# Last projection of a one-core hybrid block: residual sums and one set of weight differences from GpSimd to VectorE

## The chip, the core and the metric

One core of one Trainium2 chip runs the whole program. The metric is the device time of an execution in microseconds; the kernel before stands at the median of three runs. The engines are called by their names and, in the profile, by short ones: TensorE (PE, its weight loads PEld), VectorE (DVE), ScalarE (ACT), GpSimd (POOL) and SyncE (SP), which issues the DMAs.

## What is computed

One layer of a backbone block over 2048 tokens of width 1024 and 256 context tokens: modulation, norms, an input projection, a Fourier group beside a Mamba-2 scan, an output projection, then a SwiGLU feed-forward. Only its last line matters here, the projection back to width 1024 with a norm, a gate and a residual:

```python
def swiglu(h, w_gate, w_up, w_down):
    return (jax.nn.silu(h @ w_gate) * (h @ w_up)) @ w_down

hx2 = modulate(rms_norm(x, g_pre_ffn[l]), sf_x, cf_x)
x = x + gf_x * rms_norm(swiglu(hx2, w_gate[l], w_up[l], w_down[l]), g_post_ffn[l])
```

All of it is float32; `w_down` is 2816 x 1024.

## The kernel before, in words

**The last projection.** The tokens are worked in two pairs of blocks of 512 tokens (`PAIRS`). For each pair the product with `w_down` is a 2x2 block product done in seven multiplications instead of eight: two token blocks, two halves of the 2816, two halves of the 1024 columns. The seven are named 1 to 7, and `ORDER` gives their sequence: 1, 2, 6, 7, 4, 5, 3 for the first pair and 1, 6, 7, 4, 5, 3, 2 for the second. Below, one of these fourteen is called a position. A position has eleven steps (`f`), and a step has four token tiles of 128 with three matmuls each: operands are split into a high and a low part of a rounded type, and high x high, low x high and high x low are summed. That is 12 matmuls of 128x512 in a step and 132 in a position. The last two steps are run tile by tile.

**What a step needs.** `down_parts` makes a step's two operands up to four steps ahead (`fetch(4)`). The weight block is either a quarter of `w_down` as loaded, or a sum of quarters; it is rounded by ScalarE into `wd` and the remainder is taken by VectorE into the second half of `wd`. The hidden block comes by DMA as `hraw` (512 KB for two steps, four buffers) and is split in the same way into `hd`. So each step costs VectorE two subtractions of 128x512 and ScalarE two casts. Position 6 first changes block 11 in place to block 12 minus block 11 (`sub(G, ...)`, line 904, on GpSimd), then VectorE subtracts the outcome from block 22. Position 7 and position 4 have one difference on GpSimd in each step. In the second pair block 11 lies in the buffers `actC` (first eight steps) and `actB` (last three).

**Finishing a block of tokens.** When a block's sums are complete, `finish` (lines 1787 to 1803) norms them beside the next position: a mean square for four token tiles at once, the inverse root on GpSimd, then for each of eight half tiles of 128x512 VectorE multiplies by the inverse root and the gate (`scalar_tensor_tensor`) and GpSimd adds the saved residual `x2`. `down` draws two pieces from this generator in each step (`steps(run, 2)`, line 1871), so that it is through after six of eleven steps; then one DMA of 2048 KB stores the block. `x2` was loaded by `rows_load` in four DMAs into a buffer of `actC`. Three blocks go this way: the second block of the first pair beside the first pair's last position (here **F1**), its first block beside the second pair's first position (**F2**), and the second pair's second block beside its sixth position (**F3**). The last block ends the program in `finish_last`.

**The order.** For the last projection the order on each engine isn't the written one. The framework's scheduler arranges the instructions of each engine, and the DMAs on SyncE, by its own estimate; each engine then works through its list in that order, and an instruction that waits holds what stands behind it.

Of the kernel before, what the change touches and what calls it, by code (L numbers as in the profile page):

```python
# [17 lines left out]
ALU = mybir.AluOpType  # L18
# [143 lines left out]
def fourier_ssd_block(ctx, tc, a):  # L162
    nc = tc.nc
    pace = Pace()
    V, S, G, T = (Paced(e, n, pace) for e, n in
                  ((nc.vector, "DVE"), (nc.scalar, "ACT"), (nc.gpsimd, "POOL"), (nc.tensor, "PE")))
# [57 lines left out]
    def rsqrt_steps(ssq, n, scale, out):  # L224

        ms = sm.tile([P, n], F32, tag="rq_ms", name="rq_ms", bufs=4)
        V.tensor_scalar(ms, ssq, scale, EPS, ALU.mult, ALU.add)
        yield
        y = sm.tile([P, n], F32, tag="rq_y", name="rq_y", bufs=7)
        G.tensor_tensor(y, ms, mhalf[:, 0:n], op=ALU.pow)  # L230
        out.append(y)
        yield
# [7 lines left out]
    def steps(gen, n=99):  # L240
        for _ in range(n):
            if next(gen, 0) == 0:
                return
# [611 lines left out]
    def qslot(shape, dt=F32):  # L855
        return ff.p3.tile(list(shape), dt, tag="q", name="slot")
# [15 lines left out]
    def hidden_loads(ahead):  # L872

        while hpos[0] < min(hpos[1] + ahead + 1, 14 * ((NJ + 1) // 2)):
            pi, f2 = divmod(hpos[0], (NJ + 1) // 2)
            p, i = divmod(pi, 7)
            n = min(2, NJ - 2 * f2)
            raw = wp.tile([P, 2, 512], F32, tag="raw", name="hraw", bufs=4)
            dma(raw[:, 0:n], hgate_d[p][f2][:, 0:n, PIECE[ORDER[p][i]]])
            hraw[pi, f2] = raw  # L880
            hpos[0] += 1

    def down_parts(p, i, f):

        hpos[1] = (7 * p + i) * ((NJ + 1) // 2) + f // 2
        hidden_loads(3 if f % 2 == 0 else 2)

        def block(b):
            return wblock[p, (b, f // 4)][:, f % 4]

        def temp():
            return ta[0].tile([P, 512], F32, tag="ws", name="wt", bufs=4)

        def sub(engine, out, x, y):
            engine.tensor_tensor(out, x, y, op=ALU.subtract)
            return out

        i_ = ORDER[p][i]
        if i_ in (1, 5):
            src = block(11)  # L900
        elif i_ in (2, 3):
            src = block({2: 21, 3: 22}[i_])
        elif i_ == 6:
            sub(G, block(11), block(12), block(11))
            src = sub(V, temp(), block(22), block(11))
        elif i_ == 7:
            src = sub(G, temp(), block(22), block(12))
        else:
            src = sub(G, temp(), block(11), block(22))
            V.tensor_tensor(src, src, block(21), op=ALU.add)  # L910
        w = wp.tile([P, 2, 512], F32R, tag=("hi", "lo")[pos[1] % 2], name="wd")
        S.copy(w[:, 0], src)
        sub(V, w[:, 1], src, w[:, 0].bitcast(F32))
        raw = hraw[7 * p + i, f // 2][:, f % 2]
        tag, bufs = (("xt", 2), ("sg", 3))[pos[1] // 2 % 2]
        h = ta[0].tile([P, 2, 512], F32R, tag=tag, name="hd", bufs=bufs)
        S.copy(h[:, 0], raw)
        sub(V, h[:, 1], raw, h[:, 0].bitcast(F32))
        return w, h
# [6 lines left out]
    def next_w():  # L926
        fetch(4)
        pos[0] += 1
        return ready.pop(pos[0] - 1)
# [414 lines left out]
    with tc.manual_schedule(engines=ordered):  # L1344
# [232 lines left out]
        ff = SimpleNamespace()  # L1577
# [164 lines left out]
        run = gate_up(0, xs0, beside, last0)  # L1742
# [34 lines left out]
    half = [slice(0, 512), slice(512, D)]  # L1777
# [5 lines left out]
    def rows_load(p, r):  # L1783
        ff.x2 = act("C", F32, (P, 4, D))
        b = PAIRS[p][r]
        for t in range(4):
            dma(ff.x2[:, t], x2_d[4 * b + t])

    def finish(p, r, o, sq):

        ss = ta[0].tile([P, 4], F32, tag="fss", name="fss", bufs=2)
        V.tensor_tensor(ss, sq[:, :, 0], sq[:, :, 1], op=ALU.add)
        rs = []
        for _ in rsqrt_steps(ss, 4, 1.0 / D, rs):
            yield
        for t in range(4):
            for n in range(2):
                oh = o[:, t, half[n]]
                V.scalar_tensor_tensor(oh, oh, rs[0][:, t : t + 1], gffn[n], ALU.mult, ALU.mult)
                G.tensor_tensor(oh, oh, ff.x2[:, t, half[n]], op=ALU.add)  # L1800
                yield
        b = PAIRS[p][r]
        dma(out_d[4 * b * P : 4 * (b + 1) * P, :].rearrange("(t p) d -> p t d", p=P), o)
# [29 lines left out]
    def schedule(p):  # L1833

        at = {}
        if p == 0:
            at = {(0, 2): (0, 12, 0), (0, 5): (0, 12, 1), (0, 8): (0, 22, 0), (1, 1): (0, 22, 1), (1, 4): (0, 12, 2), (1, 7): (0, 22, 2),
                  (4, 2): (1, 11, 0), (4, 6): (1, 11, 1), (5, 2): (1, 12, 0), (5, 6): (1, 12, 1), (5, 9): (1, 11, 2),
                  (6, 0): (1, 12, 2), (6, 3): (1, 22, 0), (6, 7): (1, 22, 1)}
            rows = {(5, 4): 1, (6, 10): 0}  # L1840
        else:
            at = {(0, 3): (1, 22, 2), (1, 0): (1, 21, 2), (1, 3): (1, 21, 0), (1, 6): (1, 21, 1)}
            rows = {(4, 4): 1, (6, 2): 0}
        return at, rows

    def down(p, prev):
        at, rows = schedule(p)
        order = ORDER[p]
        run = prev
        for pos_, i in enumerate(order):  # L1850
            begin, keep = i in (1, 6, 7, 5), i in (2, 4, 3)
            if begin:
                banks = [pb.tile([P, 512], F32, tag="b", name="b") for _ in range(4)]
                if i == 1:
                    first = banks
            acc = first if i == 2 else banks
            end = p == 1 and pos_ == 6
            tail = 4 if end else 2
            f = 0
            while f < NJ:  # L1860
                m = tail if f == NJ - tail else 1
                ws = [next_w() for _ in range(m)]
                for t in range(4):
                    for df, (w, h) in enumerate(ws):
                        for n, (hi_, wi) in enumerate(((0, 0), (1, 0), (0, 1))):
                            T.matmul(acc[t], h[:, hi_, t * P : (t + 1) * P], w[:, wi], start=begin and f == 0 and n == 0,
                                     stop=f + df == NJ - 1 and n == 2, skip_group_check=keep)
                for ff_ in range(f, f + m):
                    if (pos_, ff_) in at:
                        down_load(*at[pos_, ff_])  # L1870
                    steps(run, 2)
                    if (pos_, ff_) in rows:
                        rows_load(p, rows[pos_, ff_])
                f += m
            steps(run)
            run = idle
            if i == 1:
                ff.o1 = qslot((P, 4, D))
                sq1, sq2 = (ta[0].tile([P, 4, 2], F32, tag="fsq", name="fsq", bufs=3) for _ in range(2))
            if i == 7:  # L1880
                ff.o2 = qslot((P, 4, D))
            if end:
                return finish_last(p, ff.o1, sq1, acc)
            for t in range(4):
                u1, u2 = ff.o1[:, t, half[1]], ff.o2[:, t, half[1]] if hasattr(ff, "o2") else None
                ps = acc[t]
                if i == 1:
                    S.copy(u1, ps)
                elif i == 6:
                    V.tensor_tensor(u1, u1, ps, op=ALU.add)  # L1890
                elif i == 7:
                    V.tensor_tensor(u2, u1, ps, op=ALU.add)
                elif i == 4:
                    c = ff.o2[:, t, half[0]]
                    V.tensor_tensor(c, u1, ps, op=ALU.add)
                    squares(c, sq2, t, 0)
                elif i == 5:
                    V.tensor_tensor(u2, u2, ps, op=ALU.add)
                    squares(u2, sq2, t, 1)
                elif i == 3:  # L1900
                    V.tensor_tensor(u1, u1, ps, op=ALU.add)
                    squares(u1, sq1, t, 1)
                    if p == 1:
                        V.tensor_tensor(u1, u1, gffn[1], op=ALU.mult)
                else:
                    c = ff.o1[:, t, half[0]]
                    S.copy(c, ps)
                    squares(c, sq1, t, 0)
            if i == 5:
                run = finish(p, 1, ff.o2, sq2)  # L1910
        return finish(p, 0, ff.o1, sq1)
# [27 lines left out]
```

## Time and profile before

| | |
|---|---|
| median of three runs | 2409.01 us (2407.45 to 2411.35) |
| the profiled execution | 2409.39 us, its span 2407.6 us |
| TensorE busy | 2281.4 us (95%) |
| VectorE busy | 1669.3 us (69%) |
| ScalarE busy | 1113.6 us (46%) |
| GpSimd busy | 1049.4 us (44%) |
| last projection | from 1952.44 us of the span to its end |

In the profile's views `out<-in` names the tiles that an instruction writes and reads, `x` is a count, and a bracket tells how long the engine stood idle just before and who ended that. `slot` is the tile of finished sums, `actC` holds in turn weight blocks and the residual `x2`, `b` is a PSUM bank. A row of windows gives for each engine its busy time and in brackets its instructions, then the granted TensorE clock, the DMA engines' busy share and GB/s.

### The profile page before, as it was taken

To read this page: it belongs to the slowest core of one execution; us is meant where nothing else is said; L and a number is where in the kernel's file an instruction comes from. 1 tells how busy PE (TensorE), PEld (TensorE's weight loads), DVE (VectorE), ACT (ScalarE), POOL (GpSimd) and SP (SyncE) were. 2 spreads that over 40 slices of the span, in tenths; PEclk is the share of its full clock that TensorE was granted. 3 is DMA by queue.
4 is the path that set the end of the run, shared out by engine and by line. 5 is a ranking of instruction groups with operands and counts; after the bars stand their busy time and mean duration, and the time that the engine had idled before them with its cause. 6 is when DMAs were issued, how large, how long until landed. Compare 5 with 4: busy or idle time off the path is not lost. (4 is left out here: it accounts for less than half of the span.)

```text
span 2407.6 us, 30176 instructions
## 1 busy us (share of the span) xinstructions
PE 2281.4 (95%) x10861; PEld 1865.9 (77%) x10861; DVE 1669.3 (69%) x2255; ACT 1113.6 (46%) x2017; POOL 1049.4 (44%) x667
## 2 busy tenths in 40 slices
PE   7999798999989999988999999899999999998998
PEld 3887667777778888876788888788888878876786
DVE  3559878588976888887555555855555665778666
ACT  4535453355428677765623333333323335444354
POOL 2121536635552444443454555355554541425512
PEclk9999998999999999998999999999999999999999
DMA  9355435445466888842333333433333373547333
GB/s 310 129 158 156 131 120 186 147 152 177 152 214 226 263 257 252 256 168 90 121 97 110 106 105 105 149 113 97 109 97 102 105 268 117 186 140 262 95 123 118
DMA packets 272580, 377.20 MB, mean 157 GB/s; under 512 B 17111, under 2 KB 190115, under 8 KB 269358
## 3 DMA queue, kind: packets, MB, share of 16 engines
q1 hardware_dynamic: 243062, 344.49, 44.7%
q10 hardware_dynamic: 29368, 30.78, 3.7%
q8 instruction: 86, 1.41, 0.3%
q14 instruction: 64, 0.52, 0.1%
HBM read 280.49 MB, written 94.72 MB: 156 GB/s over the span
## 5 line engine op out<-in xcount | busy, mean ns | idle before, releaser
L140 PE MATMUL b<-wd,hd 128*128 128x512 f32 x1848 | 429.5, 394 | 15.9 <-DVE hd L140 10.8
L140 PEld LDWEIGHTS b<-wd,hd 128*128 128x128 f32 x1848 | 350.1, 190 | 95.1 <-DVE hd L140 13.5
L140 PE MATMUL mm<-slot,wa 128*128 128x512 f32 x1584 | 378.6, 392 | 10.5 <-ACT sg L140 6.6
L140 PEld LDWEIGHTS mm<-slot,wa 128*128 128x128 f32 x1584 | 297.6, 189 | 75.7 <-ACT sg L140 7.4
L140 DVE SCALAR_TENSOR_TENSOR acc<-u,convw,acc 128x992 f32<-128x992 f32 (+5 forms) x228 | 310.5, 1366 | 23.5 <-ACT acc L140 19.1
L140 POOL TENSOR_TENSOR ws<-raw 128x512 f32<-128x512 f32 x88 | 127.4, 1448 | 310.3 <-DMA raw<-in_w_up_dram 131.4
L140 PE MATMUL mm<-actC,wa 128*128 128x512 f32 x984 | 241.5, 394 | 7.4 <-DVE u L140 7.2
L140 PE MATMUL mm<-actB,wa 128*128 128x512 f32 x1020 | 239.4, 390 | 0.0
L140 PE MATMUL mm<-actA,hi 128*128 128x512 f32 x704 | 227.7, 404 | 3.8 <-DVE actA L140 2.7
L140 ACT CAST wa<-ws 128x512 fp32r<-128x512 f32 x176 | 109.2, 621 | 252.9 <-PE mm L140 215.2
L140 PEld LDWEIGHTS mm<-actC,wa 128*128 128x128 f32 x984 | 186.6, 190 | 47.6 <-issue 8.7
L140 PEld LDWEIGHTS mm<-actB,wa 128*128 128x128 f32 x1020 | 191.2, 188 | 39.6
L140 DVE TENSOR_TENSOR wa<-ws,wa 128x512 fp32r<-128x512 f32 x176 | 156.9, 893 | 59.3 <-ACT wa L140 56.3
L140 POOL TENSOR_TENSOR rq_y<-rq_ms,mhalf 128x1 f32<-128x1 f32 (+2 forms) x60 | 43.1, 723 | 288.6 <-DVE rq_ms L140 274.5
L140 DVE TENSOR_TENSOR u<-u,mm 128x512 f32<-128x512 f32 x126 | 86.4, 686 | 116.4 <-PE mm L140 116.4
L140 DVE TENSOR_TENSOR wa<-raw,wa 128x512 fp32r<-128x512 f32 x132 | 118.4, 898 | 65.2 <-ACT wa L140 64.7
L140 ACT CAST wa<-raw 128x512 fp32r<-128x512 f32 x132 | 82.3, 624 | 163.1 <-PE mm L140 147.7
L140 PEld LDWEIGHTS mm<-actA,hi 128*128 128x128 f32 x704 | 130.1, 191 | 33.4 <-issue 3.7
L140 POOL TENSOR_TENSOR adacc<-adacc,adaw 128x1024 f32<-128x1024 f32 x28 | 74.1, 2648 | 181.8 <-ACT adaw L140 169.8
L140 POOL TENSOR_TENSOR lo<-raw,hi 128x1024 fp32r<-128x1024 f32 x34 | 90.2, 2652 | 128.4 <-ACT hi L140 128.4
L140 PE MATMUL mm<-actC,hi 128*128 128x512 f32 (+1 forms) x512 | 144.6, 370 | 0.0
L140 PE MATMUL mm<-actA,lo 128*128 128x512 f32 x352 | 139.2, 396 | 0.6 <-DVE lo L140 0.6
(280 smaller groups left out, 4459.1 us busy)
## 6 DMA issues: line engine op xcount, KB each, us to landing
hraw<-hg SPq DMA_DIRECT2D x70, 512.0 KB, 4.0
raw<-in_w_in_dram SPq DMA_DIRECT2D x54, 512.0 KB, 5.1
ab<-acsd SPq DMA_DIRECT2D x128, 192.0 KB, 4.8
raw<-in_w_gate_dram SPq DMA_DIRECT2D x44, 512.0 KB, 4.6
raw<-in_w_up_dram SPq DMA_DIRECT2D x44, 512.0 KB, 3.8
hg<-hs SPq DMA_DIRECT2D x22, 1024.0 KB, 5.0
adaw<-in_w_ada_dram SPq DMA_DIRECT2D x32, 512.0 KB, 3.8
l_x<-xtok SPq DMA_DIRECT2D x33, 384.0 KB, 4.2
```

The costliest lines, as they stand in the source:

```text
L140: r = issue(out, *args, **kw)
```

## The change

Three lines. In the second pair the in-place difference of position 6 is made by VectorE instead of GpSimd (eleven instructions). In `finish` VectorE adds the residual (24 instructions over F1, F2 and F3). And `down` draws one piece of `finish` in each step, so that its ten pieces and the store take all eleven steps of a position.

```diff
@@ down_parts
         elif i_ == 6:
-            sub(G, block(11), block(12), block(11))
+            sub(V if p else G, block(11), block(12), block(11))
             src = sub(V, temp(), block(22), block(11))
@@ finish
                 V.scalar_tensor_tensor(oh, oh, rs[0][:, t : t + 1], gffn[n], ALU.mult, ALU.mult)
-                G.tensor_tensor(oh, oh, ff.x2[:, t, half[n]], op=ALU.add)
+                V.tensor_tensor(oh, oh, ff.x2[:, t, half[n]], op=ALU.add)
                 yield
@@ down
                     if (pos_, ff_) in at:
                         down_load(*at[pos_, ff_])
-                    steps(run, 2)
+                    steps(run, 1)
                     if (pos_, ff_) in rows:
                         rows_load(p, rows[pos_, ff_])
```

TensorE's and ScalarE's lists are the same in both. First, VectorE's list at the start of F1, before; `fss` and `rq_ms` are the mean square, the `SCALAR_TENSOR_TENSOR` rows the multiplication by gate and root.

```order
L140 TENSOR_TENSOR fss<-fsq 128x4
L140 TENSOR_SCALAR rq_ms<-fss 128x4
L140 TENSOR_TENSOR wd<-actB,wd 128x512
L140 SCALAR_TENSOR_TENSOR slot<-slot,rq_y,gffn 128x512 x2
L140 TENSOR_TENSOR hd<-hraw,hd 128x512
L140 SCALAR_TENSOR_TENSOR slot<-slot,rq_y,gffn 128x512
L140 TENSOR_TENSOR wd<-actB,wd 128x512
L140 SCALAR_TENSOR_TENSOR slot<-slot,rq_y,gffn 128x512 x3
L140 TENSOR_TENSOR wd<-actB,wd 128x512
L140 TENSOR_TENSOR hd<-hraw,hd 128x512
```

The same place on VectorE now:

```order
L140 TENSOR_TENSOR fss<-fsq 128x4
L140 TENSOR_SCALAR rq_ms<-fss 128x4
L140 TENSOR_TENSOR wd<-actB,wd 128x512
L140 TENSOR_TENSOR hd<-hraw,hd 128x512
L140 SCALAR_TENSOR_TENSOR slot<-slot,rq_y,gffn 128x512 x2
L140 TENSOR_TENSOR slot<-slot,actC 128x512
L140 TENSOR_TENSOR wd<-actB,wd 128x512
L140 TENSOR_TENSOR slot<-slot,actC 128x512
L140 SCALAR_TENSOR_TENSOR slot<-slot,rq_y,gffn 128x512
L140 TENSOR_TENSOR hd<-hraw,hd 128x512
L140 TENSOR_TENSOR wd<-actB,wd 128x512
L140 TENSOR_TENSOR hd<-hraw,hd 128x512
```

The multiplications stand further apart, and the additions of the residual (`slot<-slot,actC`) stand between them and the splits `wd` and `hd`. GpSimd's list from F1 to the seventh product of the second pair, as a difference:

```order
-L140 TENSOR_TENSOR rq_y<-rq_ms,mhalf 128x4
-L140 TENSOR_TENSOR slot<-slot,actC 128x512 x8
-L140 TENSOR_TENSOR actC<-actA,actC 128x512 x4
-L140 TENSOR_TENSOR rq_y<-rq_ms,mhalf 128x4
-L140 TENSOR_TENSOR actC<-actA,actC 128x512
-L140 TENSOR_TENSOR slot<-slot,actC 128x512 x2
-L140 TENSOR_TENSOR actC<-actA,actC 128x512
-L140 TENSOR_TENSOR slot<-slot,actC 128x512 x3
+L140 TENSOR_TENSOR rq_y<-rq_ms,mhalf 128x4 x2
```

GpSimd keeps only the two inverse roots here. SyncE's list of DMAs from the store of F1 on, before; `hg` is the hidden block in memory, `x_178` to `x_181` are the residual rows of F2.

```order
L1803 DMA out_dram<-slot 128x4x1024
L879 DMA hraw<-hg_5597 128x2x512
L879 DMA hraw<-hg_5598 128x2x512
L879 DMA hraw<-hg_5599 128x2x512
L1787 DMA actC<-x_178 128x1024
L879 DMA hraw<-hg_5600 128x2x512
L1787 DMA actC<-x_179 128x1024
```

The same DMAs on SyncE now:

```order
L868 DMA actB<-in_w_down_dram 128x4x512
L879 DMA hraw<-hg_5597 128x2x512
L879 DMA hraw<-hg_5598 128x2x512
L868 DMA actB<-in_w_down_dram 128x4x512
L879 DMA hraw<-hg_5599 128x2x512
L879 DMA hraw<-hg_5600 128x2x512
L1803 DMA out_dram<-slot 128x4x1024
L1787 DMA actC<-x_178 128x1024
L1787 DMA actC<-x_179 128x1024
```

The store of F1 and the residual rows of F2 have moved behind four loads of the hidden block, and two loads of weights (`actB`) that stood far behind them have moved ahead.

## The prediction

> **What bounds the kernel now.** TensorE is busy for nearly the whole span, so a change pays only where TensorE stands. First the windows: each row is one position of the last projection, cut at its first matmul: an undisturbed one, F1, F2, the position after F2 (position 6 of the second pair), an undisturbed one, F3.
>
> ```profile
> core 0: us, PE busy (x) PEld busy (x) DVE busy (x) ACT busy (x) POOL busy (x), PEclk, DMA share, GB/s
> 2107.72:2137.64 29.92, 29.92 (x133) 24.78 (x132) 16.72 (x26) 15.07 (x31) 0.00 (x0) 1.00 0.53 167
> 2137.64:2170.80 33.16, 30.77 (x133) 24.55 (x132) 28.78 (x34) 13.38 (x26) 17.60 (x11) 1.00 0.41 139
> 2170.80:2214.40 43.60, 35.42 (x133) 27.69 (x132) 42.11 (x42) 17.08 (x34) 29.38 (x18) 0.88 0.70 256
> 2214.40:2244.32 29.92, 29.92 (x133) 24.78 (x132) 19.03 (x30) 12.89 (x24) 10.04 (x6) 1.00 0.52 166
> 2306.03:2335.95 29.92, 29.92 (x133) 24.77 (x132) 16.72 (x26) 15.07 (x31) 0.00 (x0) 1.00 0.50 167
> 2335.95:2367.66 31.71, 30.23 (x133) 24.70 (x132) 31.19 (x38) 15.07 (x31) 15.10 (x9) 1.00 0.41 137
> ```
>
> All hold 132 matmuls (one more is clipped). Undisturbed they take 29.92 us, 2.72 a step and 0.2267 a matmul; F1 takes 3.24 more, F2 13.68, F3 1.79: 18.71 in all, just where GpSimd adds. Next, whom TensorE waits for there (us in total, times, longest):
>
> ```profile
> PE b L140 <- DVE hd L140: 10.2, 5, 4.0
> PE b L140 <- DVE wd L140: 1.8, 1, 1.8
> PE b L140 <- DVE slot L140: 1.0, 2, 0.7
> ```
>
> It waits for VectorE's splits. The granted clock in F2, where TensorE stands longest:
>
> ```profile
> 2190.00:2195.00 5.00, 3.02 (x8) 2.21 (x9) 5.00 (x5) 0.00 (x0) 4.37 (x3) 0.81 0.00 0
> 2195.00:2200.00 5.00, 1.87 (x5) 1.09 (x4) 5.00 (x4) 0.62 (x1) 5.00 (x4) 0.84 0.00 0
> 2200.00:2205.00 5.00, 4.13 (x10) 3.29 (x11) 5.00 (x6) 0.00 (x0) 3.17 (x3) 0.50 0.53 141
> 2205.00:2210.00 5.00, 5.00 (x20) 4.04 (x19) 5.00 (x5) 2.50 (x5) 3.75 (x3) 0.83 1.02 406
> ```
>
> Here 43 matmuls took 14.02 us busy where 43 x 0.2267 = 9.75 would do: 4.27 of F2's 13.68 are clock, a consequence of the standing. Last, why VectorE is late: its timeline and GpSimd's in F1.
>
> ```profile
> 2140.88 0.16 DVE L140 TENSOR_TENSOR fss<-fsq 128x4 f32<-128x4 f32 x1
> 2141.07 0.17 DVE L140 TENSOR_SCALAR rq_ms<-fss 128x4 f32<-128x4 f32 x1
> ...
> 2142.38 1.42 DVE L140 SCALAR_TENSOR_TENSOR slot<-slot,rq_y,gffn 128x512 f32<-128x512 f32 x2 [0.22 <-POOL rq_y L140]
> ...
> 2156.52 1.77 DVE L140 TENSOR_TENSOR wd<-actB,wd 128x512 fp32r<-128x512 f32 x1
> ...
> 2160.49 0.68 DVE L140 TENSOR_TENSOR wd<-slot,wd 128x512 fp32r<-128x512 f32 x1
> 2161.09 0.68 DVE L140 TENSOR_TENSOR hd<-hraw,hd 128x512 fp32r<-128x512 f32 x1
> ```
>
> ```profile
> 2156.01 3.41 POOL L140 TENSOR_TENSOR slot<-slot,actC 128x512 f32<-128x512 f32 x2 [1.29 <-DVE slot L140]
> ```
>
> Alone, a two-input operation of VectorE lasts 0.68 and the next starts after 0.60; a multiplication takes 1.42 / 2 = 0.71. The split at 2156.52 falls under GpSimd's addition from 2156.01 and lasts 1.77: 1.1 us more. So an addition on GpSimd costs VectorE about 1.1 us, and made by VectorE itself 0.60. The Trainium skill, "SBUF — State Buffer", Who interferes with whom, says that such a two-input operation and a GpSimd one that reads SBUF share a lock held for a whole instruction. By that page an addition could cost VectorE up to GpSimd's full duration, so the gain in room would be larger than by the row; the sum below uses the row.
>
> **The change part by part.** The groups of this stretch:
>
> ```profile
> L140 POOL TENSOR_TENSOR slot<-slot,actC 128x512 f32<-128x512 f32 x24 | 40.7, 1715 | 9.0 <-DVE slot L140 8.0 <-issue 0.9
> L140 DVE SCALAR_TENSOR_TENSOR slot<-slot,rq_y,gffn 128x512 f32<-128x512 f32 x24 | 31.4, 1342 | 0.2 <-POOL rq_y L140 0.2
> L140 POOL TENSOR_TENSOR actC<-actA,actC 128x512 f32<-128x512 f32 x8 | 12.6, 1576 | 13.2 <-DVE wd L140 13.2
> L140 POOL TENSOR_TENSOR actB<-actB 128x512 f32<-128x512 f32 x3 | 5.0, 1674 | 3.1 <-DVE wd L140 3.1
> ```
>
> Removed from GpSimd: 40.7 + 12.6 + 5.0 = 58.3 us, all of it off the path by itself; what leaves the path is the 1.1 that each costs VectorE beside it. Added to VectorE: 24 + 11 operations, each 0.60 by the pitch of independent ones. Each addition follows the multiplication of the same data and may have to see it written. No row shows such a pair of 128x512; the nearest is `rq_ms` behind `fss`, which started 0.03 after the end, where independent ones start 0.08 before it. So the dependent price is at most 0.60 + 0.11 = 0.71, and I reckon with 0.71 for dependent ones. Nothing less than 0.60 is likely, for VectorE was never seen faster with two inputs of this size.
>
> F1 and F3, by the step: before, two splits 1.20, two multiplications 1.42 and two additions blocking 2.20 made 4.82 against TensorE's 2.72, for the five or six steps that `finish` lasted. Its eight additions blocked 8 x 1.1 = 8.8 us and TensorE lost 2.8 (below), so the operands made ahead covered about 6.0 us: an estimate of the lead, from these two. Now a step has 1.20 + 0.71 + 0.71 = 2.62. It fits 2.72, and over the position 16.72 + 8 x 0.71 + 8 x 0.71 = 28.1 fits 29.92. The waits go. What stays of F1's 3.24 is its beginning, where a weight load stood for the additions out of PSUM, which are in both:
>
> ```profile
> 2139.81 14.38 PEld L140 LDWEIGHTS b<-wd,hd 128*128 128x128 f32 x64 [0.40 <-DVE slot L140]
> ```
>
> I leave these 0.40: F1 gives 2.84, F3, whose beginning is smooth, 1.79.
>
> F2 is tighter, since VectorE also takes the eleven in-place differences and makes them, with the differences that follow, partly in this position and partly in the next. I sum both, 59.84 us of TensorE: 44 splits, 8 additions out of PSUM, 22 differences and 8 residual additions are 82 x 0.60 = 49.2; 8 multiplications 5.7; mean square 0.3; and 19 dependent ones (8 additions, 11 second differences) 19 x 0.11 = 2.1. That is 57.3, with 2.5 to spare and the lead of 6.0 to bridge uneven stretches. So I expect no wait of TensorE in F2, hence no lower clock either: 13.68 come off, 9.41 standing and 4.27 clock. The position after F2, which already runs at 29.92, keeps it.
>
> The DMAs move too. The store of F1 now waits for VectorE's last addition and stands, with the rows of F2 behind it, behind more loads of the hidden block, by SyncE's list.
>
> ```profile
> out_dram<-slot SPq DMA_DIRECT2D x2, 2048.0 KB
> actC<-x SPq DMA_DIRECT2D x7, 512.0 KB
> ...
> 2159.45 0.39 SPq L1803 DMA_DIRECT2D out_dram<-slot  x1
> ```
>
> ```profile
> 2180.94 2.44 DVE L140 SCALAR_TENSOR_TENSOR slot<-slot,rq_y,gffn 128x512 f32<-128x512 f32 x2
> ```
>
> Before, the store went at 2159.45, while F1 was half done. With `finish` on eleven steps I put its last addition two steps of splits from the end, near 2160.5, and the store at 2162.5, behind the load that waits for the next splits. At the 406 GB/s of the row above 2048 KB take 5.2 us and the first rows 1.3: they are there at 2169. The first addition of F2 comes after its first multiplications, which stood at 2180.94, that is 10.1 after F2's beginning; with F2 starting 2.84 earlier and some 2 us less blocking until there, near 2176. That leaves 7 us. The two moved loads of weights go into a time when the DMA share is low (0.41 in F1). SyncE's waits cost nothing by this.
>
> Sum: 2.84 + 13.68 + 1.79 = 18.31. The profiled execution takes 2409.39, which gives 2391.1; it stands 0.38 above the median of the runs, so the median should be **2390.7**. The end of the program (`finish_last`) is not touched and only comes earlier. A measurement of this kernel can tell about 0.2%, 4.8 us, from no change.
>
> **The rivals.** *VectorE itself becomes the bound in F2 and after.* It is 96% full there by my sum, and its waits for ScalarE's casts, from the waits of 2138 to 2216, aren't in it:
>
> ```profile
> ACT hd L140 <- DMA hraw<-hg: 12.1, 2, 8.6
> ...
> DVE wd L140 <- ACT wd L140: 2.6, 4, 1.0
> DVE hd L140 <- ACT hd L140: 2.5, 1, 2.5
> ```
>
> 57.3 + 2.6 + 2.5 = 62.4 is 2.6 over 59.84. If the lead doesn't bridge it, TensorE stands 2.6 us and, if the clock falls as it did, 4.27 more: 6.9 are kept, 2397.6. For it: the nearly full engine; against: the lead, and these waits came with GpSimd's blocking. 0.12. A rule speaks for it: the Trainium skill, "VectorE: DVE Perf Modes", The DRAIN you can't avoid, has each operation start only when the pipe of the one before is empty, some 0.4 us for one of 0.68. By that page VectorE would be far over its time and the kernel slower than before; the rows 0.60 apart, each lasting 0.68, speak against it here.
>
> *The hidden block comes late by DMA.* If F2's waits for `hd` are really for `hraw`, F2 keeps its 13.68 and only 4.63 come off: 2404.4, no measurable change. For it: ScalarE's casts waited for `hraw`, 12.1 in the rows above. Against: SyncE's own waits for those loads are for VectorE, so the loads were late because VectorE was:
>
> ```profile
> SPq L879 <- DVE hd L140: 42.9, 9, 18.0
> ```
>
> 0.05.
>
> *Slower: the residual rows hold VectorE.* Before, GpSimd waited for `x2` and nobody behind it mattered; now an addition whose row hasn't landed holds every split queued behind it. It decides from where a row lands more than the lead of 6.0 after its addition is due, that is 7 + 6.0 = 13.0 later than I reckon. Late by the longest wait of SyncE, 18.0, in all three finishes it would cost 3 x (18.0 - 6.0 + 4.27) = 48.8, less 18.3: 2439.5. For it: the store and 2048 KB of rows now go in one row; against: 7 us to spare and one wait of 18 in all. 0.03.
>
> My forecast has 0.80. The range goes from the forecast less the 1.6 by which the fastest run lies under the median, 2389.1, taken as 2389.0, to the first rival's, taken as 2398.0; the other two, 0.08, are left out. Faster by over 0.2%: 0.80 + 0.12 = 0.92; within: 0.05; slower: 0.03.
>
> **What would show it.** In the changed profile F1 should last about 30.3 and F2 and F3 29.9; no multiplication of `slot` should last 1.7 but all about 0.74; GpSimd's busy time should be some 58 lower; the clock in F2 should be 1.00. TensorE waiting for `hd` or `wd` in F2 with VectorE busy without a gap would speak for the first rival; casts waiting for `hraw` for the second; VectorE waiting for a DMA at `slot<-slot,actC` for the third. The prediction is wrong if F2 keeps more than 7 us.

## The result and the profile after

The changed kernel takes 2390.72 us, the median of four runs (2388.76 to 2393.55), against 2409.05 for the kernel before (four runs, 2407.45 to 2411.35): a ratio of 0.9925, 95% interval 0.9912 to 0.9937. The median is 18.33 us lower. One later execution of the changed kernel, which took 11498.75 us, is a slow one and is left out of its later median.

First the windows of the changed kernel, cut as those of before: the position that opens the last projection, then F1, F2, the position after F2, and F3. The columns are the time, and for each engine its busy time with its instructions, then the granted clock, the DMA share and GB/s.

```profile
1953.22:1987.86 34.64, 32.10 (x133) 25.82 (x132) 28.48 (x29) 14.08 (x25) 21.91 (x14) 0.95 0.79 280
...
2138.66:2168.85 30.19, 30.19 (x134) 24.70 (x132) 28.85 (x48) 15.15 (x31) 1.02 (x1) 1.00 0.58 197
2168.85:2198.77 29.92, 29.92 (x134) 24.77 (x132) 28.79 (x49) 15.40 (x30) 2.59 (x1) 1.00 0.77 281
2198.77:2228.69 29.92, 29.92 (x134) 24.77 (x132) 22.08 (x36) 12.94 (x24) 10.04 (x6) 1.00 0.64 213
...
2320.31:2350.23 29.92, 29.92 (x134) 24.78 (x132) 27.64 (x46) 15.08 (x31) 1.50 (x1) 1.00 0.49 162
```

TensorE is busy in the whole of F1, F2 and F3, at full clock. F1 has gone from 33.16 to 30.19, F2 from 43.60 to 29.92, F3 from 31.71 to 29.92: 2.97 + 13.68 + 1.79 = 18.44 us. VectorE has more instructions than before in these positions and is hardly busier for it: in F2 it was busy for 42.11 us with 42 of them, now for 28.79 with 49. GpSimd has given up all 16 additions and all eleven differences of F1 and F2 (the list ahead of the prediction stops after 13 and six of them).

Who still waits from F1 to the end of F2, in the waits of the changed kernel (us in total, times, longest):

```profile
POOL rq_y L140 <- DVE rq_ms L140: 77.6, 2, 48.5
ACT wd L140 <- PE b L140: 26.4, 19, 1.6
...
DVE wd L140 <- ACT wd L140: 1.9, 4, 0.7
...
PEld b L140 <- DVE slot L140: 0.4, 1, 0.4
```

No row has TensorE waiting for a split (`hd`, `wd`), and none has VectorE waiting for a DMA. What is left is mostly ScalarE, which waits for matmuls before it casts into `wd`. That wait is not new; it was about as long before:

```profile
ACT wd L140 <- PE b L140: 30.5, 15, 7.8
```

What has gone is TensorE's own waiting.

Last, VectorE's multiplications and additions on the tile of sums, over F1 to F3 (ns, shortest, median and longest of 24):

```profile
L140 DVE SCALAR_TENSOR_TENSOR slot<-slot,rq_y,gffn x24: 733/742/751, 2143.7 to 2340.0; 128x512 f32<-128x512 f32 x24
L140 DVE TENSOR_TENSOR slot<-slot,actC x24: 673/681/684, 2145.0 to 2341.9; 128x512 f32<-128x512 f32 x24
```

Before, the 24 multiplications took 1342 ns on average; now the longest takes 751.

### The profile page after: what moved, and what is told of

Same layout as the page of the kernel before. It is cut to its first block, busy times and chain, and to the rows that moved or that the text cites. A ratio compares the mean times of both kernels' runs of the same rounds, so it can differ in the third digit from the quotient of the medians.

```text
span 2390.1 us, 30163 instructions
## 1 busy us (share of the span) xinstructions
PE 2277.8 (95%) x10861; PEld 1868.0 (78%) x10861; DVE 1658.5 (69%) x2290; ACT 1113.7 (47%) x2017; POOL 991.4 (41%) x632
## 5 line engine op out<-in xcount | busy, mean ns | idle before, releaser
L140 PE MATMUL b<-wd,hd 128*128 128x512 f32 x1848 | 423.1, 391 | 4.1 <-ACT hd L140 1.9
```

The costliest lines, as they stand in the source:

```text
L140: r = issue(out, *args, **kw)
```

## The experiments

The theory: GpSimd's two-input operations hold up VectorE's two-input operations beside them, some 1.1 us each, and that alone made TensorE stand. The rivals: the lower pace of `finish` is what helps; the moved DMAs help; or GpSimd's being busy beside VectorE matters in some other way than through what it reads. Positions are given as F1 / F2 / F3. Before they take 33.17 / 43.59 / 31.71, now 30.19 / 29.92 / 29.92, from first matmul to first matmul (the edges of the windows are rounded, so some differ by 0.01).

**One line of the three at a time.** In the first kernel only the additions go to VectorE.

```diff
-                G.tensor_tensor(oh, oh, ff.x2[:, t, half[n]], op=ALU.add)
+                V.tensor_tensor(oh, oh, ff.x2[:, t, half[n]], op=ALU.add)
```

> VectorE adds the residual; two pieces of finish in each step and the in-place difference on GpSimd stay as before. Theory (GpSimd's two-input operations block VectorE, 1.1 us each): a step of F1 has 1.20 + 1.42 + 1.31 = 3.93 against 2.72 for five steps, 6.0 over, just covered by the lead of 6.0: F1 30 to 31, F3 30 to 31. In F2 the eleven differences still block, 12.1 us: F2 31 to 34. Total 2392 to 2397. Rival (what cost was that two pieces a step overfill VectorE, whoever adds): F1 stays at 33, F3 at 31.7, total over 2403. Rival (in F2 the differences stood behind the additions in GpSimd's queue, and that alone made them late): F2 falls to 29.9.

Measured: 2397.58 us (2393.12 to 2399.17), ratio 0.9944, interval 0.9930 to 0.9959. F1, F2 and F3 in its windows:

```profile
2139.76:2169.98 30.22, 30.22 (x134) 24.70 (x132) 27.59 (x46) 14.42 (x29) 4.38 (x3) 1.00 0.55 197
2169.98:2205.56 35.58, 31.19 (x134) 24.47 (x133) 34.88 (x45) 16.04 (x32) 15.95 (x10) 1.00 0.73 261
2327.12:2357.04 29.92, 29.92 (x134) 24.78 (x133) 27.64 (x46) 15.07 (x31) 1.50 (x1) 1.00 0.51 168
```

Where GpSimd has nothing left to add (F1, F3) the position is as short as in the changed kernel, without the new pace. F2, where GpSimd still makes the in-place differences (15.95 us busy), keeps 5.65 of its 13.68. F2's 35.57 is above the 31 to 34 expected, and the total lies just above its expected range. F2 did not fall to 29.9, so the order of GpSimd's queue alone doesn't explain it.

In the second kernel only the pace changes.

```diff
-                    steps(run, 2)
+                    steps(run, 1)
```

> One piece of finish in each step; additions and differences stay on GpSimd. Blocking theory: a step of F1 has 1.20 + 0.71 + 1.1 = 3.01, 0.29 over 2.72, for eight steps 2.3 over, covered by the lead: F1 30.3, F3 29.9. In F2 and the position after it VectorE needs 63 x 0.60 + 5.7 + 0.3 + 19 x 1.1 = 64.7 against 59.84, 4.9 over, of which the lead bridges most: F2 30 to 33. Total 2391 to 2395. Rival (pace alone): F2 29.9 too, total 2391. If the engine alone mattered and the pace not at all: F1 33, F2 43, total 2409.

Measured: 2406.80 us (2403.35 to 2408.73), ratio 0.9990, interval 0.9981 to 0.9999; 31.83 / 41.81 / 31.89. I had expected the pace to do much of the work, and it does 2 us. VectorE's timeline and GpSimd's in its F1 show why:

```profile
2142.47 3.11 DVE L140 SCALAR_TENSOR_TENSOR slot<-slot,rq_y,gffn 128x512 f32<-128x512 f32 x3
2145.51 1.78 DVE L140 TENSOR_TENSOR wd<-actB,wd 128x512 fp32r<-128x512 f32 x1
2147.21 1.77 DVE L140 TENSOR_TENSOR hd<-hraw,hd 128x512 fp32r<-128x512 f32 x1
2148.91 1.40 DVE L140 SCALAR_TENSOR_TENSOR slot<-slot,rq_y,gffn 128x512 f32<-128x512 f32 x2
2150.23 1.78 DVE L140 TENSOR_TENSOR wd<-actB,wd 128x512 fp32r<-128x512 f32 x1
```

```profile
2149.73 3.44 POOL L140 TENSOR_TENSOR slot<-slot,actC 128x512 f32<-128x512 f32 x2 [1.29 <-DVE slot L140]
...
2159.17 1.67 POOL L140 TENSOR_TENSOR slot<-slot,actC 128x512 f32<-128x512 f32 x1 [1.29 <-DVE slot L140]
```

The text asks for one piece in a step; the scheduler still puts two and three multiplications together, and GpSimd's last addition ends at 2160.84, about three quarters through F1. A step's two splits and two multiplications, from 2145.51 to 2150.23, take 4.72 us against TensorE's 2.72. My expectation of 2391 to 2395 had worked with the written order, and missed. In this kernel too the store (at 2161.99) and the rows behind it go out after more loads, and F2 still takes 41.81.

In the third kernel only the second pair's in-place differences go to VectorE.

```diff
-            sub(G, block(11), block(12), block(11))
+            sub(V if p else G, block(11), block(12), block(11))
```

> Only the in-place difference of the second pair goes to VectorE. Blocking theory: F1 33.2 and F3 31.7 as before, since nothing changes there; F2 loses eleven blocks of 1.1 and gains eleven operations of 0.60 to 0.71, some 5 us less for VectorE: F2 34 to 39, with part of the clock's 4.27. Total 2400 to 2405. Rival (queue order on GpSimd made F2 late): F2 29.9, total 2395.

Measured: 2404.68 us (2402.89 to 2406.52), ratio 0.9979, interval 0.9969 to 0.9989; 33.17 / 37.85 / 31.71. F1 and F3 are those of before, F2 is 5.74 shorter.

**Two of the three.** The fourth kernel has the additions and the differences but draws two pieces in each step; the fifth has the additions and the pace without the differences.

> Additions and differences on VectorE, but two pieces of finish in each step. Blocking theory: F1 and F3 30 to 31 as with the additions alone; F2 and the next position need 57.3 against 59.84, but the load comes in the first six steps: F2 29.9 to 32. Total 2391 to 2394. Rival (pace): F1 stays at 33, F3 at 31.7, F2 over 36, total over 2403.

> The additions on VectorE and one piece of finish in each step, the in-place difference of the second pair on GpSimd. Blocking theory: F1 and F3 as in the changed kernel, 30.2 and 29.9; F2 keeps what the eleven differences block, as it did with the additions alone (35.6): 33 to 36. Rival (with a slower pace the differences find room): F2 29.9 to 31.

Measured without the pace: 2392.02 us (2390.79 to 2394.06), ratio 0.9924, interval 0.9907 to 0.9940; 30.19 / 29.92 / 29.92, the changed kernel's positions to the last digit. Without the differences, one run: 2398.73 us; 30.19 / 34.14 / 29.92, and 0.22 more in the position after F2. So the additions and the differences simply add up: the additions give 12.75 (33.17 + 43.59 + 31.71 less 30.23 + 35.57 + 29.92), the differences 5.74 alone or 5.65 on top of the additions (35.57 to 29.92). Together 18.4 to 18.5, which is what there was to gain. The pace gives 2.9 where GpSimd adds (1.34 in F1, 1.78 in F2, -0.18 in F3), 1.25 on top of the additions (1.43 in F2 less 0.22 after it, 0.04 in F1), and nothing once GpSimd is quiet.

**Is it what GpSimd reads?** Three kernels take the changed one, whose lists on TensorE, VectorE and ScalarE they keep, and give GpSimd back useless work: 24 pieces on residual half tiles that have already been added. The first kind reads and writes, as the additions did:

```diff
                 V.tensor_tensor(oh, oh, ff.x2[:, t, half[n]], op=ALU.add)
+                G.tensor_tensor(ff.x2[:, t, half[n]], ff.x2[:, t, half[n]], gffn[n], op=ALU.mult)
```

The second only writes the same half tile, `G.memset(ff.x2[:, t, half[n]], 0.0)`; the third does that three times over, to be as long as the multiplication.

> The changed kernel, and after each addition of the residual GpSimd multiplies the used half tile of residual rows by the gate, in place, which nobody reads: 24 more operations on GpSimd that read and write SBUF. The lists of TensorE, VectorE and ScalarE are the same. Blocking theory: each costs VectorE 1.1; F1 needs 28.1 + 8.8 = 36.9 of VectorE against 29.92: F1 and F3 33 to 37, F2 34 to 44 with the clock. VectorE's operations beside them last 1.7. Rival (VectorE's load, its order and its waits for GpSimd's results made the difference, not the sharing): F1 30.2, F2 and F3 29.9 as in the changed kernel, for no engine waits for these operations.

> The same, but GpSimd fills the used half tile with zeros instead: as many operations with the same waits, which write SBUF and read nothing. Blocking theory, if only GpSimd's reading blocks VectorE's second input: F1 30.2, F2 and F3 29.9, VectorE's operations 0.68. If any operation of GpSimd blocks: as with the extra reading, in proportion to how long a fill lasts.

> As with the extra writing, but each half tile is filled three times, so that GpSimd is busy about as long (3 x 0.53 = 1.6 us) as with the extra reading (1.7 us). If GpSimd's reading of SBUF is what blocks VectorE's second input: F1 30.2, F2 and F3 29.9, all of VectorE's operations 0.68 or 0.74. If the length of GpSimd's work decides and a fill was only too short to matter: F1 33 to 36, F3 32 to 35, with operations of VectorE at 1.7 or at 1.2.

Measured with the reading work, one run: 2409.55 us, so that what the change had gained is gone (before took 2409.84 beside it). Its windows of F1, F2, the position after and F3:

```profile
2139.82:2175.52 35.70, 32.15 (x133) 25.79 (x132) 35.16 (x45) 13.57 (x27) 16.28 (x9) 0.95 0.44 137
2175.52:2210.84 35.32, 32.40 (x134) 25.80 (x132) 35.22 (x48) 16.87 (x34) 14.53 (x9) 0.95 0.64 234
2210.84:2241.36 30.52, 30.21 (x133) 24.70 (x132) 30.13 (x41) 12.92 (x24) 13.50 (x7) 1.00 0.69 232
2333.18:2367.82 34.64, 31.87 (x134) 25.82 (x132) 34.16 (x44) 13.97 (x29) 17.41 (x9) 0.95 0.35 116
```

In the positions 16.2 of the 18.44 us are back (5.51 + 5.40 + 0.60 + 4.72 over the changed kernel's); F1 also begins 1.16 later, which isn't the work's doing, since the work begins after that. Nobody uses what GpSimd computes there, so no wait for an outcome can carry the delay, and SyncE's order around the store of F1 is the changed kernel's, so the moved DMAs alone can't have made the gain. GpSimd's timeline and VectorE's show what carries it:

```profile
2157.56 3.38 POOL L140 TENSOR_TENSOR actC<-actC,gffn 128x512 f32<-128x512 f32 x2 [2.43 <-DVE slot L140]
```

```profile
2156.80 1.28 DVE L140 TENSOR_TENSOR slot<-slot,actC 128x512 f32<-128x512 f32 x2
2158.01 1.77 DVE L140 TENSOR_TENSOR wd<-slot,wd 128x512 fp32r<-128x512 f32 x1
2159.70 1.78 DVE L140 TENSOR_TENSOR hd<-hraw,hd 128x512 fp32r<-128x512 f32 x1
2161.41 1.40 DVE L140 SCALAR_TENSOR_TENSOR slot<-slot,rq_y,gffn 128x512 f32<-128x512 f32 x2
```

Two operations of GpSimd, 3.38 / 2 = 1.69 each, and beside them exactly two of VectorE, which start 1.69 apart instead of 0.60: one turn each. The difference, 1.09, is the price of 1.1 that the prediction read off one row.

Measured with the writing work, one run each: 2393.87 us and, three times as long, 2393.57 us. The longer one's windows of F1, F2 and F3, and a stretch of GpSimd and of VectorE:

```profile
2140.26:2170.44 30.18, 30.18 (x133) 24.70 (x132) 28.85 (x48) 15.15 (x31) 13.42 (x25) 1.00 0.59 193
2170.44:2200.36 29.92, 29.92 (x133) 24.77 (x132) 28.78 (x49) 15.41 (x30) 14.95 (x25) 1.00 0.78 284
2321.94:2351.86 29.92, 29.92 (x133) 24.78 (x132) 27.61 (x46) 15.08 (x31) 13.99 (x25) 1.00 0.51 163
```

```profile
2154.77 3.11 POOL L140 MEMSET actC<- 128x512 f32 x6 [1.43 <-DVE slot L140]
```

```profile
2154.03 1.28 DVE L140 TENSOR_TENSOR slot<-slot,actC 128x512 f32<-128x512 f32 x2
2155.24 0.68 DVE L140 TENSOR_TENSOR wd<-slot,wd 128x512 fp32r<-128x512 f32 x1
2155.84 0.68 DVE L140 TENSOR_TENSOR hd<-hraw,hd 128x512 fp32r<-128x512 f32 x1
2156.44 1.41 DVE L140 SCALAR_TENSOR_TENSOR slot<-slot,rq_y,gffn 128x512 f32<-128x512 f32 x2
```

GpSimd is about as busy as with the reading work (13.42 and 14.95 us in F1 and F2, against 16.28 and 14.53), at the same places, and VectorE and TensorE don't notice: 0.68 an operation, positions of 30.18, 29.92, 29.92. The 3 us by which the two single times lie over the changed kernel's median aren't in these positions; F1 begins 1.6 and 1.9 us later in these executions. So it is GpSimd's reading, not its being busy, that holds VectorE. An operation of GpSimd that reads only one tile was not tried. The Trainium skill, "SBUF — State Buffer", Who interferes with whom, says just this: two SBUF inputs on VectorE contend with a GpSimd instruction that reads SBUF, not with one that only writes. The trace agrees on both halves: 1.77 beside the reading work, 0.68 beside the fills.

**Do the residual rows matter?** The changed kernel with F2's rows loaded three times over, which fills the queue and has them land later.

```diff
-        for t in range(4):
-            dma(ff.x2[:, t], x2_d[4 * b + t])
+        for t in range(4 * 3 if (p, r) == (0, 0) else 4):
+            dma(ff.x2[:, t % 4], x2_d[4 * b + t % 4])
```

> The changed kernel, with the residual rows of F2 loaded three times over, so that the last landing is 2 x 5.2 = 10.4 us later and the loads of the hidden block behind them too. The scheduler answers by moving the additions of F2 behind more splits. If late rows hold VectorE as the rival of the prediction has it: VectorE waits for a DMA at an addition and TensorE stands in F2 for what goes beyond the lead, F2 31 to 45. If the rows have 7 us to spare and the scheduler's order bridges the rest: F2 29.9 to 31.

Measured, one run: 2390.22 us; 30.23 / 31.35 / 29.92. Its window of F2, the waits of TensorE and VectorE there, and VectorE's first addition:

```profile
2165.38:2196.72 31.34, 30.21 (x133) 24.70 (x132) 30.20 (x51) 15.03 (x30) 2.59 (x1) 1.00 0.91 343
```

```profile
DVE wd L140 <- ACT wd L140: 12.6, 13, 1.4
...
PE b L140 <- DVE hd L140: 1.1, 1, 1.1
```

```profile
2184.70 1.28 DVE L140 TENSOR_TENSOR slot<-slot,actC 128x512 f32<-128x512 f32 x2
```

The DMA share is 0.91 and the first addition comes 19.3 us after F2's beginning, against 8.1 in the changed kernel (2176.96 - 2168.85, row below). Yet VectorE never waits for a DMA: the scheduler knew of the extra loads and put the additions further back, behind splits and differences. F2 is 1.4 us longer, just above the 29.9 to 31 expected for rows that are in time; that the bunched additions cost it is likely, since TensorE waits 1.1 for a split there, but not shown. What a row costs that lands late against the scheduler's estimate isn't shown by this; a kernel with late rows and an unchanged order wasn't tried.

**The same step taken further.** In the first pair GpSimd still makes the in-place differences of position 6, and the scheduler puts several of them into the opening position (34.64 above), where GpSimd is 21.91 us busy and the clock is 0.95. Position 4 of both pairs, the one that makes product 4 (31.11 and 31.51), has a difference on GpSimd in each step. Two kernels move these too, measured beside the changed kernel and the one before:

```diff
-            sub(V if p else G, block(11), block(12), block(11))
+            sub(V, block(11), block(12), block(11))
```

and, in the second of them as well,

```diff
-            src = sub(G, temp(), block(11), block(22))
+            src = sub(V, temp(), block(11), block(22))
```

> The changed kernel once more, beside the next two on the same chip: 2390 to 2393.

> The in-place difference goes to VectorE in the first pair too. There GpSimd makes four of these differences ahead of the last sums of the hidden block, which TensorE waits for at the first position (34.6 against 29.92). By the blocking theory and GpSimd's queue the first position falls to 31 to 33.5 and nothing else moves: 1.5 to 3.5 us faster than the changed kernel, 2388 to 2390. Rival (VectorE's own list is as full there, and the sums wait for it instead): no difference, 2391, or a little slower.

> As the one before, and the first difference of product 4 on VectorE in both pairs, so that a step there has four operations of VectorE, 2.4 of 2.72 us. Its position takes 31.1 and 31.5 in the changed kernel, where TensorE stands for the additions out of PSUM that are queued behind blocked splits. Blocking theory: these fall to 30 to 31, another 0.5 to 2.5 us less, 2386 to 2389. Rival (the additions out of PSUM are late by VectorE's order alone): these two positions stay, and with the fuller engine the total is that of the one before or slower.

Measured: before 2410.03; changed 2390.14 (2388.19 to 2394.29), ratio 0.9920, interval 0.9907 to 0.9934; position 6 on VectorE in both pairs 2386.39 (2384.73 to 2389.14), ratio 0.9903, interval 0.9890 to 0.9917; position 4 as well 2385.62 (2384.52 to 2386.82), ratio 0.9898, interval 0.9883 to 0.9913. The opening position with the first edit:

```profile
1950.41:1981.84 31.43, 30.22 (x134) 24.70 (x133) 26.39 (x40) 14.30 (x25) 3.83 (x2) 1.00 0.92 321
```

and the opening position and the two position 4 with both:

```profile
1953.76:1984.86 31.10, 30.24 (x133) 24.70 (x132) 26.35 (x40) 14.29 (x25) 3.23 (x2) 1.00 0.93 324
2074.62:2104.54 29.92, 29.92 (x133) 24.77 (x132) 22.38 (x36) 13.89 (x27) 0.00 (x0) 1.00 0.66 220
2254.68:2284.88 30.20, 30.20 (x133) 24.70 (x132) 22.47 (x36) 13.90 (x27) 0.00 (x0) 1.00 0.34 96
```

The opening position loses 3.21 with the first edit, and with the second the two others lose 1.19 and 1.31. The 2.5 us of these two are GpSimd's differences gone from beside VectorE; they show in the positions, while the two kernels' times overlap. The first edit's 3.75 us between medians is more than the 1.5 to 3.5 expected, and its runs overlap those of the changed kernel too. What it does in the opening position isn't shown to be sharing alone. GpSimd also makes the last sums of the hidden block there, behind its differences, and TensorE waits 1.9 us for the cast of these sums in the changed kernel and no longer here. Nor is the opening position the same in every execution: in twelve kernels that leave its instructions alone it takes 34.20 to 35.01, but 32.25 in one of them (the longer writing work).

## Why the prediction was right

Its three terms, against what the positions measured: F1 2.84, measured 2.97; F2 13.68, measured 13.68; F3 1.79, measured 1.79. F2 and F3 agree to the last digit because both were forecast to fall to the 29.92 of an undisturbed position, and did. That the median comes within 0.02 us of the forecast is luck, for the four runs are spread over 4.8 us. In the profiled executions the span falls a little less than 18.44, from 2407.6 to 2390.1, since the last projection begins 0.78 later (1953.22 against 1952.44) and its opening position is 0.23 longer (34.64 against 34.41): 18.44 - 0.78 - 0.23 = 17.43.

- *GpSimd's additions cost VectorE 1.1 each.* Shown: given back as useless reads they bring the standing back, as writes they don't. The price was 1.09 out of GpSimd's 1.69, not the full duration that the prediction named as the dearer possibility. Without them VectorE's operations are at 0.68 and 0.74, as forecast. GpSimd's busy time was to fall by some 58; the page of the changed kernel has it at 991.4 where it was 1049.4:

```profile
PE 2277.8 (95%) x10861; PEld 1868.0 (78%) x10861; DVE 1658.5 (69%) x2290; ACT 1113.7 (47%) x2017; POOL 991.4 (41%) x632
```

  VectorE, with 35 instructions more, is 10.8 less busy (1669.3 before).
- *The clock is a consequence of the standing.* What was clock came off with the rest; F2 has 1.00. With the reading work the standing came back, and the clock in F1 fell to 0.95. Not every standing lowers it: with the additions alone F2 takes 35.58 at 1.00. The split of the 13.68 was rough, for TensorE was idle for 43.60 - 35.42 = 8.18 of F2, not 9.41; since both parts came off, the sum is the same.
- *The lead of 6.0.* This term was not confirmed, and the sum didn't need it. With the reading work VectorE needed 36.9 us in F1 (28.1 + 8.8), 7.0 over 29.92, and F1 still grew by 5.8, so little more than 1 was bridged. The 6.0 had been taken from the blocking that cost TensorE nothing; but before the change VectorE had about 7 us free in F1 anyway (29.92 less 16.72, 5.7 and 0.3), which is enough to account for it.
- *What F1 keeps.* The weight load that waits 0.40 for the additions out of PSUM is still in the waits; F1 keeps 0.27 over 29.92 where 0.40 was left in. That is the whole miss of this term.
- *Dependent operations start 0.71 apart.* VectorE's timeline before F2 has one such pair, the in-place difference and the one that reads it:

```profile
2162.76 0.69 DVE L140 TENSOR_TENSOR actC<-actA,actC 128x512 f32<-128x512 f32 x1
2163.47 0.69 DVE L140 TENSOR_TENSOR wt<-actA,actC 128x512 f32<-128x512 f32 x1
...
2176.36 0.68 DVE L140 TENSOR_TENSOR wd<-actC,wd 128x512 fp32r<-128x512 f32 x1
2176.96 0.68 DVE L140 TENSOR_TENSOR slot<-slot,actC 128x512 f32<-128x512 f32 x1
```

  0.71 it is in this pair, but few paid it: the scheduler mostly puts a split between, and then the pitch is 0.60.
- *VectorE is 96% full in F2 and the position after.* Too full a figure: 57.3 us were summed, 28.79 + 22.08 = 50.87 were measured, 85% of 59.84. The two windows hold 85 instructions where I counted 92. Four of the others went into F1, which has 48 where 26 of an undisturbed position and 18 of `finish` make 44: pairs like that at 2162.76, in a position that was thought to be taken up by its own work. And most dependent operations didn't pay the 0.11.
- *The moved store and rows.* The store was put at 2162.5, the first addition of F2 near 2176. SyncE's timeline has the store at 2163.44, and the addition stands above at 2176.96, without a wait:

```profile
2163.44 0.60 SPq L1803 DMA_DIRECT2D out_dram<-slot  x1
```

  The rows had less to spare than the 7 us reckoned. The third of the four, issued at 2166.26, landed 10.4 later, at 2176.6; at the prediction's 1.3 each the first landed near 2174, an estimate, some 3 us before its addition.
- *VectorE itself becomes the bound.* It did not: in F2 it is busy for 28.79 of 29.92, waits 1.9 for the casts in F1 and F2 together, and TensorE never waits for it there. The rule that spoke for this rival, from the Trainium skill, "VectorE: DVE Perf Modes", The DRAIN you can't avoid, has the next operation start only when the pipe is empty, but its first paragraph adds that an operation that isn't held starts earlier, which the prediction left out. The rows above, each 0.68 long and 0.60 apart, fit the addition: independent operations of this kind paid no such gap here.
- *The hidden block comes late by DMA.* It did not: F2 lost all 13.68, and no cast there waits for `hraw`. Over F1 and F2 SyncE's waits for VectorE's splits fell from 42.9 us to 24.3, the longest from 18.0 to 7.3, which fits that the loads had been late because VectorE was.
- *The residual rows hold VectorE.* Not seen. Its mechanism, a row later than the scheduler expects, stays untested.

One thing the prediction did not say, since its sum didn't need it: which of the three lines does what. The additions give about 12.8, the differences 5.7, and the pace nothing that the other two don't give.

## What to carry to other kernels

Before giving VectorE's work to an idle GpSimd, compare the durations of VectorE's two-input operations with and without a GpSimd operation beside them: here one on GpSimd cost VectorE 1.1 us, while VectorE does it itself in 0.60. An engine that is busy all the time may in part be held up, and taking on more work itself can make it less busy: VectorE was busy for 42.11 of F2's 43.60 us with 42 instructions, and for 28.79 with 49. It matters only where VectorE is short of room: the position after F2 keeps six GpSimd differences, 10.04 us, and runs at 29.92, with VectorE busy for 22.08. And where a scheduler arranges the instructions, a pace written into the source is a wish: read the order that came out.

## What the hardware showed beyond what was expected

GpSimd's fills are harmless to VectorE at any length tried: six in a row, 3.11 us, left the operations beside them at 0.68. Where both engines run on, the delay is mostly shared out in turns, one operation of VectorE for each of GpSimd, so a run of GpSimd operations slows VectorE to the 1.69 that one of them takes. GpSimd pays too: a two-input operation of this size lasts 1.26 where VectorE stands idle (at 1961.48 in the changed kernel). And not every meeting goes GpSimd's way: with the reading work two of its operations from 2163.49 took 4.54 us, while three of VectorE's (2163.34, 2163.94, 2164.54) went by 0.60 apart. What decides who goes first wasn't tested. The multiplication by a per-token value (`SCALAR_TENSOR_TENSOR`, also two tiles read) is held in the same way: with GpSimd's additions and differences gone the longest of 24 is 751 ns, where the mean was 1342.
